# Sixteen product steps ahead of the gate matrices, their low halves by TensorE and ScalarE, and four of eight scaled one-hots on VectorE

## The chip, the cores and the metric

One of the eight cores of a Trainium2 chip runs the whole program. The metric is the device time of one execution in microseconds. The kernel before takes 2879.54 us (median of three runs, 2871.32 to 2884.39). The profiled execution, from which all rows are taken, took 2871.9 us.

## The reference, cut to what matters

A decoder block: two convolutional token mixers and a projection, then a layer of 16,384 single-neuron experts (PEER) for 1024 tokens of width 1024. Each token picks 16 experts for each of 8 heads, from the sums of two scores over 128 keys each.

```python
idx = e1 * PEER_N_KEYS + e2
gates = jax.nn.softmax(vals.astype(jnp.float32), axis=-1).astype(q.dtype)
u_sel = jnp.take(u, idx, axis=0)
act = jax.nn.gelu(jnp.einsum("chkd,cd->chk", u_sel, xc))
v_sel = jnp.take(v, idx, axis=0)
return jnp.einsum("chk,chkd->cd", act * gates, v_sel)
```

## The kernel before, in words

The front part makes the mixers, the normed tokens and, in `front`, the routing: VectorE picks the best 16 of 128 scores for every token and head. The tokens stand in eight tiles of 128. Three tiles are done by gathering: their experts' rows of u and v are fetched one by one. Five tiles (`ND`, 640 tokens) are done densely: all 128 chunks of 128 experts are multiplied with all 640 tokens, and a gate matrix, 0 where an expert was not picked, weighs the result.

`gate_matrix` makes these gates for a token as one product of two one-hot matrices: 128 picks by the 128 first keys, scaled with the gates (`o1`), and 128 picks by the 128 second keys (`o2`). It goes through each tile in 16 blocks of 8 tokens (`W`). For a block VectorE writes `o2` for all eight tokens (line 691, reading the transposed picks from PSUM). For the first `X` = 6 tokens VectorE writes unscaled bf16 one-hots `ob` (line 693), and ScalarE scales each token's by its gates (line 698). For the other two VectorE makes the scaled one-hot itself (line 700). TensorE multiplies (line 705; an fp32 product is two records in the trace), ScalarE copies the 128x512 result into `st` (line 708), and after 64 tokens SyncE stores `st` in DRAM, four transfers each. `o1`, `o2`, `ob`, `st`, `pa` have two buffers each, and so has the PSUM pool of the results (`pmm`). Ahead of a tile's blocks TensorE transposes its picks (lines 676, 678), and VectorE and ScalarE make the next tile's (`experts`, lines 498 to 535).

Beside the gates, TensorE makes the u products of 16 of the 128 chunks (`AHEAD`). `hidden_ahead` is a generator: a chunk is four steps (two halves of the width, two column ranges of 320 tokens), each of 12 products in three terms, high by high, low by high and high by low (`mm3`, lines 186 to 188). `prep_u` loads a chunk's u rows, transposes them on TensorE (line 733, PSUM pool `ptr`, two banks), ScalarE rounds them to the high half `uhi` (line 154), and VectorE subtracts that from the PSUM bank for the low half `ulo` (line 155). Behind a finished column range stands a Gelu on ScalarE (line 757) and a store (line 758). `gate_matrix` takes `LEAD` = 4 of the generator's steps before tile 0, 0.6 of a step (`RATE`) with each block of 8 tokens, and what is left after the last block:

```python
ahead, due = self.hidden_ahead(gm), 0.0
for _ in range(LEAD):
    next(ahead)
...
due += RATE
while due >= 1:
    next(ahead, None)
    due -= 1
...
for _ in ahead:
    pass
```

Then `token_experts` makes the picks of the three gathered tiles (line 545), and `dense` does the other 112 chunks with the gathered tiles' fetches between them. The gates are read back for two chunks at a time (line 801).

The program's order is not the order of the source: a scheduler puts each engine's instructions into one queue by priorities and expected readiness, and each queue is then taken strictly in that order. The products ahead use the four PSUM banks of pool `pms`, two for a chunk; the routing's scores and each tile's transposed picks use the same four.

Of the kernel before, what the change touches and what calls it, by code (L numbers as in the profile page):

```python
# [10 lines left out]
F32 = mybir.dt.float32  # L11
F32R = mybir.dt.float32r
# [9 lines left out]
P = 128  # L22
# [20 lines left out]
GB_T = 64  # L43
GB, LAG = 8, 6
AHEAD = list(range(5, NK, 8))
# [2 lines left out]
STEP = 4  # L48
AHD = 1
PACE = (2, 2, 2, 2, 1, 1, 1, 1, 1, 1)  # L50
LEAD = 4
HEAD = 4


def segments(n):
    m = -(-n // 512)
    step = -(-n // m)
    step += step % 2
    return [slice(i, min(i + step, n)) for i in range(0, n, step)]


class Block:
# [28 lines left out]
    def constants(self):  # L91
        nc, t, const = self.nc, self.t, self.const
        self.ident = self.tile(const, [P, P], F32, "ident")
        make_identity(nc, self.ident)
        self.identb = self.tile(const, [P, P], BF16, "identb")
        nc.scalar.copy(self.identb, self.ident)
        self.ones = self.tile(const, [P, P], F32, "ones")
        nc.vector.memset(self.ones, 1.0 / C)
        nrow = SCW + CFW + 5
        with self.pool("vec", 1) as vec:  # L100
            rows = self.tile(vec, [P, C], F32, "rows")
            nc.scalar.dma_start(rows[0:SCW], t["sc_conv_w"][0])
            nc.scalar.dma_start(rows[SCW:SCW + CFW], t["cf_conv_w"][0])
            for i, k in enumerate(("cf_conv_b", "cf_ln_g", "cf_ln_b", "out_norm_g_sc", "out_norm_g_cf")):
                r = SCW + CFW + i
                nc.scalar.dma_start(rows[r:r + 1], t[k][0:1])
            self.cols = self.tile(const, [P, 4, nrow], F32, "cols")
            ps = self.tile(self.ptr, [P, 4, P], F32, "tr")
            for c in range(4):
                nc.tensor.transpose(ps[:, c, :nrow], rows[:nrow, c * P:(c + 1) * P], self.ident[:nrow, :nrow])  # L110
            nc.vector.tensor_copy(self.cols, ps[:, :, :nrow])
        self.h_d = self.tile(self.dram, [SEQ, D], F32, "hd")
        self.x_d = self.tile(self.dram, [NG * P, D], F32, "xd")
        self.p_d = self.tile(self.dram, [len(AHEAD), P, ND * P], F32, "pd")
        self.g_d = self.tile(self.dram, [NK // 2, NK, ND * P // GB_T, 2, GB_T], F32, "gd")
# [538 lines left out]
    def gate_matrix(self, first, routes):  # L654

        nc, V = self.nc, self.nc.vector
        W, X, B = 8, 6, GB_T
        with self.pool("gm", 2, right=True) as gm:
            iota = self.tile(gm, [P, NK], F32, "iota", bufs=1)
            nc.gpsimd.iota(iota, pattern=[[1, NK]], base=0, channel_multiplier=0,  # L660
# [5 lines left out]
# [3 lines that stand above are left out]
            for n in range(ND):  # L669
# [4 lines left out]
                for l in range(2):  # L674
                    for m in range(TOPK):
                        nc.tensor.matmul(ps[:, l, :], oh[:, l * TOPK + m], self.identb,
                                         start=m == 0, stop=m == TOPK - 1)
# [7 lines left out]
                for q in range(P // W):  # L685
                    with self.tc.high_priority(offset=400 if n == 0 and q < HEAD else 0):
# [8 lines left out]
                        for m in range(W):  # L695
                            c = W * q + m
# [5 lines left out]
                        for z in range(W // 4):  # L702
                            pg = self.tile(self.pmm, [P, 512], F32, "mm").rearrange("p (e t) -> p e t", t=4)
                            for m in range(4):
                                nc.tensor.matmul(pg[:, :, m], o2[:, 4 * z + m, :], o1[:, 4 * z + m, :],  # L705
                                                 start=True, stop=True)
                            c = (W * q + 4 * z) % B
# [19 lines left out]
    def prep_u(self, c, q):  # L727
# [7 lines left out]
        self.split(*uT, ps)  # L735
        return uT

    def hidden(self, ps, uT, q, s):

        (hi, lo), (xh, xl) = uT, self.nT  # L740
        self.mm3(ps, (lambda a: hi[:, a, :], lambda a: lo[:, a, :]), (lambda b: xh[:, b, s], lambda b: xl[:, b, s]),
                 [(k, 4 * q + k) for k in range(4)], q == 0, q == 1)

    def hidden_ahead(self, pool):

        T = ND * P
        segs = segments(T)
        uT = self.prep_u(AHEAD[0], 0)
        for i, c in enumerate(AHEAD):
            pu = [self.tile(self.pms, [P, 512], F32, "ms")[:, :s.stop - s.start] for s in segs]  # L750
            for q in range(2):
                cur = uT
                for s, ps in zip(segs, pu):
                    self.hidden(ps, cur, q, s)
                    if q == 1:
                        p = self.tile(pool, [P, segs[0].stop], F32, "pa")[:, :s.stop - s.start]
                        self.nc.scalar.activation(p, ps, AF.Gelu_apprx_tanh)
                        self.nc.sync.dma_start(self.p_d[i, :, s], p)
                    if s is segs[0]:
                        if q == 0:  # L760
                            uT = self.prep_u(c, 1)
                        elif i + 1 < len(AHEAD):
                            uT = self.prep_u(AHEAD[i + 1], 0)
                    yield

    def dense(self, stream):
# [111 lines left out]
```

## Time and profile before

| | us |
|---|---|
| median of three runs | 2879.54 |
| profiled execution | 2871.9 |
| its span, first to last instruction | 2870.1 |
| TensorE busy (matmul records) | 2712.1 (94%) |
| TensorE weight loads | 2485.9 (87%) |
| VectorE busy | 2434.9 (85%) |
| ScalarE busy | 945.3 (33%) |
| GpSimd busy | 919.0 (32%) |

Busy shares are means over stages with different limits, so a stage is read in a view of windows. In the views PE is TensorE, PEld its weight loads, DVE VectorE, ACT ScalarE, POOL GpSimd and SP SyncE; PEclk is the clock that TensorE was granted as a share of full speed (2.4 GHz, or half of it, 1.2 GHz). A row of the timeline gives the start, the time taken by a run of equal instructions (xcount) and, in brackets, the idle time of the engine before it with what ended it. Matmul ends are modelled, so what a product costs in a burst is read from start to start.

### The profile page before, as it was taken

The numbers are of one execution on the slowest core, as the hardware profiler recorded it, in microseconds if no ns is written. First come the engines' busy times: TensorE is split into PE (matmuls) and PEld (weight loads), VectorE is DVE, ScalarE is ACT, GpSimd is POOL, SyncE is SP. The second block draws the span as 40 slices with busy tenths as digits, with TensorE's granted clock in tenths as the row PEclk, the third lists the DMA queues.
The fourth block names the chain that finished last, engine by engine and source line by source line (L and its number), as shares of the span: only waits on it lengthen the run. The fifth ranks groups of instructions, "written<-read, shape, count | busy, mean of one in ns | idle before, by whom it ended". The sixth has DMA issues, their size and how long they took to land.

```text
span 2870.1 us, 43789 instructions
## 1 busy us (share of the span) xinstructions
PE 2712.1 (94%) x16481; PEld 2485.9 (87%) x16481; DVE 2434.9 (85%) x5024; ACT 945.3 (33%) x1887; POOL 919.0 (32%) x793
## 2 busy tenths in 40 slices
PE   6999999986999989999999999999999999999998
PEld 6999989976888988898888889888888889888887
DVE  5998777998777569889889898889899988989986
ACT  4112431116999731222222212222222222222222
POOL 0000011110000025445544454445544544545440
PEclk9999999998999999999999999999999999999999
DMA  3112221101656789999989999999999999989992
GB/s 112 45 45 82 95 96 37 38 19 43 181 163 174 211 315 325 329 321 332 324 311 319 320 331 334 321 329 326 333 326 325 326 327 319 326 316 333 330 313 82
DMA packets 299540, 684.08 MB, mean 238 GB/s; under 512 B 20617, under 2 KB 153737, under 8 KB 299328
## 3 DMA queue, kind: packets, MB, share of 16 engines
q0 software_dynamic: 110592, 402.70, 39.4%
q1 hardware_dynamic: 188256, 276.92, 28.9%
q8 instruction: 130, 2.13, 0.3%
q10 hardware_dynamic: 480, 1.65, 0.1%
q14 instruction: 82, 0.67, 0.1%
HBM read 624.05 MB, written 57.15 MB: 237 GB/s over the span
## 4 chain that ended last, share of the span: by engine, by line
PE 64%; DVE 16%; ACT 9%; DMA 9%; issue 2%; SPq 0%; DVEq 0%; ACTq 0%
PE ms L188 12%; PE ms L187 12%; PE ms L186 12%; PE mm L188 7%; PE mm L186 7%; PE mm L187 7%; DMA raw<-in_peer_v_dram 7%; ACT o L698 4%; DVE row L637 3%; PE tr L733 2%; PE mm L705 2%; DVE vlo L155 2%; ACT st L708 2%; DVE g L611 1%; DVE s L467 1%
## 5 line engine op out<-in xcount | busy, mean ns | idle before, releaser
L588 POOL DMA_INDIRECT g<-in_peer_u_dram,ix x384 | 435.1, 1133 | 831.1 <-DVE ix L549 391.1
L186 PE MATMUL mm<-nhi,uhi 128*128 128x320 f32 x1792 | 573.1, 320 | 32.4 <-ACT p L824 32.0
L588 POOL DMA_INDIRECT g<-in_peer_v_dram,ix x384 | 440.6, 1147 | 455.1 <-DVE row L637 387.6
L188 PE MATMUL mm<-nhi,ulo 128*128 128x320 f32 x1792 | 557.7, 312 | 15.7 <-DVE ulo L155 15.1
L187 PE MATMUL mm<-nlo,uhi 128*128 128x320 f32 x1792 | 554.7, 310 | 0.0
L186 PE MATMUL ms<-vhi,phi 128*128 128x512 f32 x1280 | 501.4, 392 | 1.5 <-ACT phi L154 1.4
L188 PE MATMUL ms<-vhi,plo 128*128 128x512 f32 x1280 | 498.8, 390 | 0.0
L187 PE MATMUL ms<-vlo,phi 128*128 128x512 f32 x1280 | 498.7, 390 | 0.0
L637 DVE SCALAR_TENSOR_TENSOR row<-g,w,row 128x1024 f32<-128x1024 f32 x384 | 492.0, 1281 | 6.1 <-DMA row<-hd 4.7
L611 DVE SCALAR_TENSOR_TENSOR g<-g,row 128x1024 f32<-128x1024 f32 x384 | 464.5, 1222 | 0.0
L186 PEld LDWEIGHTS mm<-nhi,uhi 128*128 128x128 f32 x1792 | 338.4, 189 | 42.4 <-ACT p L824 40.3
L188 PEld LDWEIGHTS mm<-nhi,ulo 128*128 128x128 f32 x1792 | 337.5, 188 | 24.9 <-DVE ulo L155 23.9
L187 PEld LDWEIGHTS mm<-nlo,uhi 128*128 128x128 f32 x1792 | 338.7, 189 | 1.2
L154 ACT CAST phi<-p 128x320 fp32r<-128x320 f32 x256 | 116.4, 459 | 561.6 <-PE ms L187 340.8
L186 PEld LDWEIGHTS ms<-vhi,phi 128*128 128x128 f32 x1280 | 240.5, 188 | 51.0 <-ACT phi L154 2.4
L188 PEld LDWEIGHTS ms<-vhi,plo 128*128 128x128 f32 x1280 | 240.5, 188 | 50.6 <-DVE plo L155 0.5
L154 ACT CAST vhi<-raw 128x1024 fp32r<-128x1024 f32 x128 | 132.9, 1049 | 456.7 <-PE ms L188 316.5
L187 PEld LDWEIGHTS ms<-vlo,phi 128*128 128x128 f32 x1280 | 240.6, 188 | 49.0
L791 DVE TENSOR_TENSOR acc<-acc,ms 128x512 f32<-128x512 f32 x320 | 219.4, 685 | 34.7 <-PE ms L188 33.9
L155 DVE TENSOR_TENSOR ulo<-tr,uhi 128x512 fp32r<-128x512 f32 x256 | 175.4, 687 | 52.7 <-ACT uhi L154 51.8
L155 POOL TENSOR_TENSOR wlo<-wraw,whi 128x1024 fp32r<-128x1024 f32 x16 | 38.0, 2378 | 568.6 <-ACT whi L154 568.6
L154 ACT CAST uhi<-tr 128x512 fp32r<-128x512 f32 x256 | 149.4, 584 | 198.3 <-PE tr L733 195.9
(201 smaller groups left out, 4978.5 us busy)
## 6 DMA issues: line engine op xcount, KB each, us to landing
raw<-in_peer_u_dram SPq DMA_DIRECT2D x128, 512.0 KB
raw<-in_peer_v_dram SPq DMA_DIRECT2D x128, 512.0 KB
gd<-st SPq DMA_DIRECT2D x40, 1024.0 KB
g<-gd SPq DMA_DIRECT2D x64, 640.0 KB
wraw<-in_w_in_dram SPq DMA_DIRECT2D x20, 512.0 KB
wraw<-in_peer_w_q_dram SPq DMA_DIRECT2D x16, 512.0 KB
g<-in_peer_u_dram,ix POOLq DMA_INDIRECT x384
g<-in_peer_v_dram,ix POOLq DMA_INDIRECT x384
```

Source lines behind the costliest of these rows:

```text
L154: nc.scalar.copy(hi, src)
L155: self.mark(eng.tensor_tensor(lo, src, hi.bitcast(F32), op=OP.subtract))
L186: self.nc.tensor.matmul(ps, lh(a), rh(b), start=first and i == 0, stop=False)
L187: self.nc.tensor.matmul(ps, lh(a), rl(b), start=False, stop=False)
L188: last = self.nc.tensor.matmul(ps, ll(a), rh(b), start=False, stop=final and i == n - 1)
L588: self.nc.gpsimd.indirect_dma_start(out=g, out_offset=None, in_=self.t[table][0], in_offset=bass.IndirectOffsetOnAxis(ap=ix, axis=0))
L611: self.after(nc.vector.scalar_tensor_tensor(ut, ut, 1.0, b["x"], op0=OP.mult, op1=OP.mult, accum_out=b["act"][:, k:k + 1]))
L637: self.after(nc.vector.scalar_tensor_tensor(b["h"], b.pop(k), res[0][:, k:k + 1], b["h"], op0=OP.mult, op1=OP.add))
L698: nc.scalar.activation(o1[:, m, :], ob[:, :, m], AF.Copy, scale=eT[:, 2, c:c + 1])
L705: nc.tensor.matmul(pg[:, :, m], o2[:, 4 * z + m, :], o1[:, 4 * z + m, :], start=True, stop=True)
L708: nc.scalar.copy(st[:, :, c:c + 4], pg)
L791: self.mark(V.tensor_tensor(acc[:, i, dd], acc[:, i, dd], po, op=OP.add))
```

## The change

`LEAD` becomes 16, four whole chunks. The chunks ahead are prepared by a new function, `prep_ahead`: the same four transposes into a PSUM bank, ScalarE's rounded copy `uhi`, then a product of `uhi` with a negative identity that TensorE adds onto the same bank, so that the bank holds the low half, and a second ScalarE copy for `ulo`. VectorE has no part in it. `prep_u` stays as it is for the dense stage. And `X` becomes 4: of eight tokens ScalarE scales four, VectorE makes four, and `ob` has 512 columns where it had 768.

```diff
--- before.py
+++ after.py
@@ -48,7 +48,7 @@
 STEP = 4
 AHD = 1
 PACE = (2, 2, 2, 2, 1, 1, 1, 1, 1, 1)
-LEAD = 4
+LEAD = 16
 HEAD = 4
 
 
@@ -94,6 +94,8 @@
         make_identity(nc, self.ident)
         self.identb = self.tile(const, [P, P], BF16, "identb")
         nc.scalar.copy(self.identb, self.ident)
+        self.minus = self.tile(const, [P, P], F32R, "minus")
+        nc.scalar.mul(self.minus, self.ident, -1.0)
         self.ones = self.tile(const, [P, P], F32, "ones")
         nc.vector.memset(self.ones, 1.0 / C)
         nrow = SCW + CFW + 5
@@ -654,7 +656,7 @@
     def gate_matrix(self, first, routes):
 
         nc, V = self.nc, self.nc.vector
-        W, X, B = 8, 6, GB_T
+        W, X, B = 8, 4, GB_T
         with self.pool("gm", 2, right=True) as gm:
             iota = self.tile(gm, [P, NK], F32, "iota", bufs=1)
             nc.gpsimd.iota(iota, pattern=[[1, NK]], base=0, channel_multiplier=0,
@@ -735,6 +737,22 @@
         self.split(*uT, ps)
         return uT
 
+    def prep_ahead(self, c, q):
+
+        nc = self.nc
+        if q == 0:
+            self.raw = self.load("peer_u", c)
+        ps = self.tile(self.ptr, [P, 4, P], F32, "tr")
+        for k in range(4):
+            nc.tensor.matmul(ps[:, k, :], self.raw[:, (4 * q + k) * P:(4 * q + k + 1) * P], self.ident,
+                             is_transpose=True, start=k == 0, stop=k == 3)
+        hi, lo = (self.tile(self.de, [P, 4, P], F32R, "u" + s, bufs=3) for s in ("hi", "lo"))
+        flat = lambda x: x.rearrange("p a b -> p (a b)")
+        nc.scalar.copy(hi, ps)
+        nc.tensor.matmul(flat(ps), self.minus, flat(hi), start=False, stop=True, skip_group_check=True)
+        nc.scalar.copy(lo, ps)
+        return hi, lo
+
     def hidden(self, ps, uT, q, s):
 
         (hi, lo), (xh, xl) = uT, self.nT
@@ -745,7 +763,7 @@
 
         T = ND * P
         segs = segments(T)
-        uT = self.prep_u(AHEAD[0], 0)
+        uT = self.prep_ahead(AHEAD[0], 0)
         for i, c in enumerate(AHEAD):
             pu = [self.tile(self.pms, [P, 512], F32, "ms")[:, :s.stop - s.start] for s in segs]
             for q in range(2):
@@ -758,9 +776,9 @@
                         self.nc.sync.dma_start(self.p_d[i, :, s], p)
                     if s is segs[0]:
                         if q == 0:
-                            uT = self.prep_u(c, 1)
+                            uT = self.prep_ahead(c, 1)
                         elif i + 1 < len(AHEAD):
-                            uT = self.prep_u(AHEAD[i + 1], 0)
+                            uT = self.prep_ahead(AHEAD[i + 1], 0)
                     yield
 
     def dense(self, stream):
```

What the scheduler makes of it is shown at three places. Lines from 96 on are two to eighteen higher in the changed file: 676 became 678, 698 became 700, 705 became 707, 733 became 747 in `prep_ahead`, 757 became 775.

TensorE where tile 0's gates begin; `tr` are the transposed u, `ms` the banks of the products or of the transposed picks, `oh` the picks of tile 0. Before:

```order
L733 MATMUL tr_6635<-ident_75,raw_6633 128x128 x4
L733 MATMUL tr_6658<-ident_75,raw_6633 128x128 x4
L186 MATMUL ms_6644<-nhi_110,uhi_6640 128x320
L187 MATMUL ms_6644<-nlo_111,uhi_6640 128x320
L186 MATMUL ms_6645<-nhi_110,uhi_6640 128x320
L187 MATMUL ms_6645<-nlo_111,uhi_6640 128x320
L676 LDWEIGHTS oh_6426
L676 MATMUL ms_6348<-identb_80,oh_6426 128x128
```

and now, the end of the four chunks and the first transposes of the picks:

```order
L188 MATMUL ms_6882<-nhi_112,uhi_6900 128x320
L189 MATMUL ms_6882<-nlo_113,uhi_6900 128x320
L190 MATMUL ms_6882<-nhi_112,ulo_6901 128x320
L678 LDWEIGHTS oh_6428
L678 MATMUL ms_6350<-identb_80,oh_6428 128x128
```

Before, four of the first chunk's products stood ahead of the transposes of tile 0's picks, the other 44 behind. Now all 192 products of four chunks stand ahead, between the same score products of the routing and the same transposes.

ScalarE at the same place; `lst` and `pos` are what the picks of a tile are made from, `pi` and `pj` come from VectorE, `eT` are tile 0's transposed picks. Before:

```order
L518 CAST pos_6423<-pj_6405 128x8x16
L515 CAST lst_6772<-ind_439_3679 128x2x8x16
L682 COPY eT_6789<-ms_6348 128x384
L684 CAST e1b_6791<-ms_6348 128x128
L530 ACTIVATE gate_6781<-gate_6781 128x128
L517 CAST pos_6774<-pi_6755 128x8x16
L698 ACTIVATE o_926_6795<-ob_6797,eT_6789 128x128 x2
```

and now:

```order
L517 CAST lst_7011<-ind_440_3681 128x2x8x16
L751 CAST uhi_6822<-tr_6817 128x512
L519 CAST pos_7013<-pi_6994 128x8x16
L775 ACT_TABLE_LOAD
L775 ACTIVATE pa_6695<-ms_6647 128x320
L775 ACTIVATE pa_6722<-ms_6648 128x320
L753 CAST ulo_6823<-tr_6817 128x512
L751 CAST uhi_6861<-tr_6856 128x512
L520 CAST pos_7013<-pj_6995 128x8x16
L532 ACT_TABLE_LOAD
L532 ACTIVATE gate_7020<-gate_7020 128x128
L775 ACT_TABLE_LOAD
```

The cast from `pi_6994` (tile 1's positions, VectorE's) stands ahead of the first chunk's two Gelus, of a low half for the third chunk and of a high half for the fourth; between here and `eT` the order switches the table seven times. Outside this place the numbers of ScalarE's scaled one-hots fall from 480 to 320 and VectorE's rise from 160 to 320.

TensorE at the end of the gate stage; `mm` with `o` are gate matrices, `mm` with `identb` the picks of the first gathered tile. Before:

```order
L705 MATMUL mm_9984<-o_1509_9972,o_1508_9971 128x128
L705 MATMUL mm_9990<-o_1509_9972,o_1508_9971 128x128 x4
L187 MATMUL ms_10015<-nlo_111,uhi_9967 128x320
L188 MATMUL ms_10015<-nhi_110,ulo_9968 128x320
L186 MATMUL ms_10015<-nhi_110,uhi_9967 128x320
```

and now:

```order
L707 MATMUL mm_10235<-o_1539_10223,o_1538_10222 128x128
L189 MATMUL ms_10097<-nlo_113,uhi_10115 128x320
L707 MATMUL mm_10241<-o_1539_10223,o_1538_10222 128x128
L190 MATMUL ms_10097<-nhi_112,ulo_10116 128x320
L707 MATMUL mm_10241<-o_1539_10223,o_1538_10222 128x128 x3
L547 LDWEIGHTS identb_80
L547 MATMUL mm_10303<-oh_10291,identb_80 128x128
```

Before, 140 products and their transposes of u follow the last gate matrix, ahead of line 545. Now the last products of the sixteenth chunk alternate with the last gate matrices, and line 547 (545 before) follows at once. From there on the queues are the same in both programs but for single places.

## Rows read from the trace of the kernel before

**Rows 1.** Windows of the four stretches around the change: length, busy time of each engine

```profile
core 0: us, PE busy (x) PEld busy (x) DVE busy (x) ACT busy (x) POOL busy (x), PEclk, DMA share, GB/s
646.00:675.00 29.00, 9.34 (x54) 8.61 (x55) 27.33 (x181) 7.58 (x11) 0.00 (x0) 0.62 0.13 43
...
675.00:985.00 310.00, 289.64 (x2134) 263.50 (x2133) 235.47 (x472) 302.30 (x734) 0.00 (x0) 0.99 0.55 156
985.00:1008.00 23.00, 22.52 (x157) 21.97 (x155) 3.46 (x5) 5.23 (x11) 0.00 (x0) 1.00 1.00 295
1008.00:1033.00 25.00, 16.99 (x152) 16.24 (x152) 15.98 (x16) 9.19 (x14) 3.84 (x3) 0.80 0.82 305
```

**Rows 2.** ACT groups from 676 to 1010 us: xcount, busy us, mean ns, idle before

```profile
L698 ACT ACTIVATE o<-ob,eT 128x128 f32<-128x128 bf16 x480 | 186.2, 470 | 2.4 <-DVE ob L693 2.2
...
L154 ACT CAST uhi<-tr 128x512 fp32r<-128x512 f32 x30 | 17.6, 591 | 6.0 <-PE tr L733 6.0
...
L757 ACT ACT_TABLE_LOAD x6 | 7.7, 1283 | 0.1
```

**Rows 3.** Waits in the gate stage: who waited for whom, us, times, longest

```profile
DVE ob L693 <- ACT o L698: 41.4, 38, 2.5
PEld mm L705 <- ACT o L698: 23.3, 53, 1.9
```

**Rows 4.** Timeline of PE at the routing's end: start, us, what, idle before

```profile
646.21 1.94 PE L733 MATMUL tr<-ident,raw 128*128 128x128 f32 x8 [3.79 <-DMA raw<-in_peer_u_dram]
...
663.70 3.50 PE L676 MATMUL ms<-identb,oh 128*128 128x128 bf16 x32 [14.24 <-DVE s L467]
...
672.53 0.64 PE L188 MATMUL ms<-nhi,ulo 128*128 128x320 f32 x1 [5.21 <-DVE ulo L155]
```

**Rows 5.** Timeline of DVE at the same place and in the stage

```profile
671.79 0.69 DVE L155 TENSOR_TENSOR ulo<-tr,uhi 128x512 fp32r<-128x512 f32 x1
...
672.52 0.68 DVE L155 TENSOR_TENSOR ulo<-tr,uhi 128x512 fp32r<-128x512 f32 x1
...
674.67 0.29 DVE L502 SCALAR_TENSOR_TENSOR pi<-slot,pi 128x128 f32<-128x128 uint16 x1
...
675.12 2.35 DVE L691 TENSOR_TENSOR o<-iota,ms 128x1024 f32<-128x1024 f32 x2
...
698.50 1.11 DVE L700 TENSOR_SCALAR o<-iota,eT 128x128 f32<-128x128 f32 x4
699.52 1.02 DVE L693 TENSOR_TENSOR ob<-iob,e1b 128x768 bf16<-128x768 bf16 x2
```

**Rows 6.** Timeline of ACT at the start of the gate stage

```profile
675.04 0.76 ACT L517 CAST pos<-pi 128x128 bf16<-128x128 f32 x1
678.04 4.42 ACT L698 ACTIVATE o<-ob,eT 128x128 f32<-128x128 bf16 x12 [2.23 <-DVE ob L693]
682.34 0.58 ACT L708 COPY st<-mm 128x512 f32<-128x512 f32 x1
682.94 1.28 ACT L757 ACT_TABLE_LOAD   x1
684.23 0.44 ACT L757 ACTIVATE pa<-ms 128x320 f32<-128x320 f32 x1
```

**Rows 7.** Timeline of PE, last gate matrices and half a chunk of the tail

```profile
978.76 2.99 PE L705 MATMUL mm<-o,o 128*128 128x128 f32 x24
981.50 0.39 PE L186 MATMUL ms<-nhi,uhi 128*128 128x320 f32 x1
...
989.52 0.60 PE L733 MATMUL tr<-ident,raw 128*128 128x128 f32 x4
...
993.48 0.60 PE L733 MATMUL tr<-ident,raw 128*128 128x128 f32 x4
```

**Rows 8.** Timeline of SP's queue: the last gates' store and first read

```profile
985.29 10.58 SPq L716 DMA_DIRECT2D gd<-st  x4
...
1001.25 0.41 SPq L801 DMA_DIRECT2D g<-gd  x1
```

## The prediction

> **What bounds the kernel now.** I read the trace by stages first. The program has four stretches around the change [rows 1]: the end of the routing, 646 to 675 us, in which VectorE is busy (27.3 of 29.0 us), TensorE nearly idle (9.3 us) and its granted clock 0.62 of full speed; the gate stage, 675 to 985 us; a tail, 985 to 1008 us, in which TensorE alone works (22.5 of 23.0 us, VectorE 3.5, ScalarE 5.2); and from 1008 to 1033 us the experts of the last three tiles, before the dense stage. What follows, to 2870 us, has the same instructions before and after, so what the four stretches give is what the kernel gives.
>
> In the gate stage ScalarE is busy for 302.3 of 310 us [rows 1], 97.5%. TensorE shows 289.6 us, but its ends are modelled; VectorE shows 235.5 us. The costliest ScalarE group says with what: 480 scaled one-hots (line 698) [rows 2]. The waits agree: VectorE stands 41.4 us because ScalarE has not yet read a one-hot buffer, TensorE's weight loads stand 23.3 us for a scaled one-hot [rows 3]. ScalarE bounds this stage, TensorE bounds the tail, VectorE bounds the routing's end.
>
> **The routing's end.** TensorE has the first u chunk at 646.21, then stands 14.24 us until VectorE frees a PSUM bank for the gates' transposes, and 5.21 us more for the low half of u, a VectorE subtraction queued behind the routing [rows 4]. VectorE reaches its two subtractions at 671.79 and 672.52 [rows 5]. The change gives the low halves to TensorE and ScalarE, and puts four chunks where one stood. So 3 more chunks fill an idle TensorE. But queues are in order: the gates of tile 0 now stand behind all four chunks on TensorE, and on ScalarE the Gelus of the chunks stand behind a cast that waits for VectorE (second piece of order in the change's section).
>
> When does the gate stage begin? The source of that cast is ready at 674.67 + 0.29 [rows 5], less the two subtractions that go (0.60 us each from start to start): 673.5. From there ScalarE has in its order 2 position casts of 0.76 us, 8 Gelus and, priced like them, 3 exponentials of 0.44 [rows 6], 7 table loads of 1.28 and 7 casts of 0.59 [rows 2]: 1.5 + 4.8 + 9.0 + 4.1 = 19.4 us, to 693. TensorE needs these results, so it ends its chunks there, transposes the gates (3.5 us for 32 before [rows 4], some of it beside), and the first comparison starts near 695, where it started at 675.12 [rows 5]. **Term 1: +20 us.** Bounds: half a chunk (24 products, 4 transposes) takes 3.96 us when nothing else runs [rows 7], so eight take 32 us at full clock, to 678, with the transposes 682, +7; at half clock throughout, 63 + 3.5 us from 646, to 713, +38. I take the ScalarE sum, since its rows are nearest, and it lies between.
>
> The price of a table load I take as the trace has it: the copy before it starts at 682.34 and takes 0.58, the load starts at 682.94, the Gelu follows at 684.23 [rows 6], nothing else between. The Trainium skill (ScalarE: Activation LUTs, What ACT_TABLE_LOAD costs) puts a switch at about 2.66 us, 1.28 for the load and 1.38 for a drain; the load agrees, the drain shows in no row here. By that price the start would come 7 x 1.38 = 9.7 us later still, and the sum below would be 20 us instead of 30.
>
> **The gate stage.** Per eight tokens, two scaled one-hots leave ScalarE, two come to VectorE.
> - ScalarE: 12 of them took 4.30 us from start to start [rows 6], 0.36 each; 160 go: -57. 24 low-half copies come in the stage (the other 8 lie before it), priced as the high-half casts, 0.59 [rows 2], less some overlap: +13. About 3 table loads and some casts move ahead: -8. 302 becomes 250 us.
> - VectorE: four scaled one-hots took 1.02 us from start to start [rows 5], 0.255 each; 160 come: +41. The subtractions go (24 x 0.6: -14), routing work pulled ahead -9, and the bf16 one-hot over 512 columns instead of 768 (0.51 us each [rows 5]) saves between nothing and a third, 0 to 13. 235 becomes 240 to 253 us.
> - TensorE: 24 records (12 matrices) started in 2.74 us [rows 7], 0.228 each: 640 take 146. Twelve chunks of 7.9 us: 95. Gate transposes 8. The 24 subtractions by a negative identity are not in the trace; bounded by a 128x320 product and two of them (half a chunk's 3.96 us over 28 gives 0.14, so 0.14 to 0.28), near the upper for their 512 columns: 6. Sum 255 us.
>
> So the three engines come out at 250, 245 and 255, and none carries the stage alone. Bounds of its length: 257, if ScalarE is filled as it is now (250 / 0.975); 310, if the lighter ScalarE turns into waits elsewhere. I take **283**, where the engines are filled to 88 to 90%: below today's 97.5%, which one engine reached while the other two had a fifth or more to spare. **Term 2: -27 us.**
>
> **The tail.** 16 chunks are 64 steps. The stage advances 0.6 step per eight tokens, 48 steps for 640 tokens; before, 4 + 48 leave 12 steps, three chunks, for the tail; now 16 + 48 leave none, and the first expert transposes stand right behind the last gate matrix (third piece of order). **Term 3: -23 us** [rows 1].
>
> What hid behind the tail: the store of the last gates (10.58 us of issue from 985.29) and the first read of them, issued at 1001.25, 16 us after [rows 8]. Now their cover is the 25 us in which the three tiles' experts are made [rows 1]. That is enough, so they cost nothing. Were it not there, 16 us would come back. The negative identity at the start is one ScalarE instruction beside loads.
>
> **Sum.** 20 - 27 - 23 = **-30 us**. Against the profiled execution's 2871.9 us that is 2842. That execution lies 7.6 us below the median of the runs, 2879.5; the same change from the median gives **2850 us**.
>
> **The rivals.**
> - *Interlock.* With one-hots, gate banks and transposed blocks in two buffers each, three equally loaded engines wait for each other in turn. For it: 41.4 us of VectorE's waits already come from one two-deep buffer [rows 3]. Against it: TensorE has hidden products to put between. The stage takes 300 us, the sum is 20 - 10 - 23 = -13: 2866.
> - *The lead blocks the gates* (slower). TensorE takes its queue in order, so the gates can't start until four chunks, each with two round trips through ScalarE for hi and lo, are done. With the clock at the 0.62 of that stretch or below, start +38, and if then the stage is no shorter, +38 - 23 = +15: 2894. It decides once start and stage together exceed today's 333 us (675 to 1008). Against it: it takes the worst of both bounds.
> - *Better than forecast.* The start comes at +10, the stage runs in 262: 10 - 48 - 23 = -61: 2818.
>
> **How the numbers follow.** My forecast (20 to 45 us gained) 0.62; interlock 0.22 (6 to 20 us gained); the blocked start 0.07; better 0.09. A measurement can tell about 0.5%, 14.4 us, from no change. All of the forecast, the better case, and a third of the interlock lie beyond it: faster 0.78. The rest of the interlock and the milder blocked starts: same 0.17. Slower 0.05. The range takes terms 1 and 2 about half-way to their bounds: 13 - 40 - 23 = -50, 2830; 28 - 8 - 23 = -3, 2876.
>
> **What would show it.** Right: first comparison near 695; ScalarE below 92% in the gate stage, VectorE at 85% or more; last gate copy near 978, the expert transposes directly behind it, and every later event some 30 us earlier. Wrong: a start beyond 705; a stage over 300 us with all three engines below 85%; a read of the gates that the dense stage waits for; or a dense stage that has itself become longer.

## The result, and the profile after

The changed kernel takes **2841.96 us** (median of 4 runs, 2834.92 to 2844.79), the kernel before 2877.38 us beside it (median of 4): ratio **0.9868, interval 0.9847 to 0.9890**. The forecast was 2850, range 2830 to 2876, faster by over 0.5%. The time is inside, but two terms of the sum are off by 9 to 13 us, with opposite signs. The profiled execution (span 2838.8 us, before 2870.1) shows it.

Windows of the changed kernel in the columns of [rows 1]: the end of the routing with the lead, the gate stage, the experts with the start of the dense stage.

```profile
core 0: us, PE busy (x) PEld busy (x) DVE busy (x) ACT busy (x) POOL busy (x), PEclk, DMA share, GB/s
648.00:698.00 50.00, 43.78 (x275) 40.01 (x276) 33.26 (x208) 29.93 (x46) 0.00 (x0) 0.89 0.25 83
698.00:968.00 270.00, 265.58 (x2101) 252.95 (x2100) 240.84 (x576) 237.63 (x585) 0.00 (x0) 1.00 0.63 178
968.00:1004.00 36.00, 21.45 (x186) 20.15 (x183) 15.50 (x18) 9.03 (x16) 8.28 (x8) 0.85 0.99 333
```

The gate stage is 270 us instead of 310. ScalarE fell from 302 to 238 us, VectorE shows 241, and TensorE is busy for 265.6 of 270: 98%. There is no tail. In the third row the transfers are busy all the time (0.99), and TensorE works for 21 of 36 us.

TensorE's timeline around the end of the gates (start, duration, what, idle time before it and its releaser):

```profile
967.31 0.83 PE L707 MATMUL mm<-o,o 128*128 128x128 f32 x6
967.98 1.95 PE L547 MATMUL mm<-oh,identb 128*128 128x128 bf16 x32
...
983.46 3.24 PE L547 MATMUL mm<-oh,identb 128*128 128x128 bf16 x32 [4.13 <-DVE oh L526]
...
1005.38 1.09 PE L735 MATMUL tr<-ident,raw 128*128 128x128 f32 x4 [7.89 <-DMA raw<-in_peer_u_dram]
```

The experts' transposes (line 547) stand directly behind the last gate matrix, at 967.98 where they stood at 1008.13, 40.2 us earlier; what lay between, half a chunk at a time, is in [rows 7]. The span is only 31.3 us shorter. The last row shows most of the difference: TensorE stands 7.89 us for a chunk of u that has not arrived, a wait that the kernel before does not have.

The first comparison of VectorE, and ScalarE's queue ahead of it:

```profile
698.56 2.35 DVE L693 TENSOR_TENSOR o<-iota,ms 128x1024 f32<-128x1024 f32 x2
```

```profile
675.75 0.59 ACT L751 CAST uhi<-tr 128x512 fp32r<-128x512 f32 x1 [11.32 <-PE ms L189]
676.26 0.77 ACT L519 CAST pos<-pi 128x128 bf16<-128x128 f32 x1
677.05 1.28 ACT L775 ACT_TABLE_LOAD   x1
678.34 0.77 ACT L775 ACTIVATE pa<-ms 128x320 f32<-128x320 f32 x2
...
680.75 1.28 ACT L532 ACT_TABLE_LOAD   x1
682.05 0.31 ACT L532 ACTIVATE gate<-gate 128x128 f32<-128x128 f32 x1
...
697.48 0.48 ACT L684 COPY eT<-ms 128x384 f32<-128x384 f32 x1 [1.18 <-PE ms L680]
```

The start is 23.4 us later than in [rows 5]. The lead's first transpose is itself 2.0 us later (648.23 against 646.21 [rows 4]), a difference that lies ahead of the change; so the change moved the start by 21.4.

The gate stage's groups of the changed kernel (count, busy us, mean ns, idle before), one engine after the other:

```profile
L707 PE MATMUL mm<-o,o 128*128 128x128 f32 x1280 | 180.1, 282 | 4.0 <-ACT st L710 2.2 <-ACT o L700 1.5 <-DVE o L702 0.2
...
L752 PE MATMUL tr<-uhi,minus 128*128 128x512 f32 x23 | 10.9, 475 | 0.2 <-ACT uhi L751 0.2
```

```profile
L700 ACT ACTIVATE o<-ob,eT 128x128 f32<-128x128 bf16 x320 | 108.2, 408 | 1.9 <-PE mm L707 1.7
L710 ACT COPY st<-mm 128x512 f32<-128x512 f32 x159 | 90.5, 588 | 17.3 <-PE mm L707 16.9
```

```profile
L693 DVE TENSOR_TENSOR o<-iota,ms 128x1024 f32<-128x1024 f32 x80 | 97.1, 1219 | 11.5 <-PE mm L707 10.1
L702 DVE TENSOR_SCALAR o<-iota,eT 128x128 f32<-128x128 f32 x320 | 87.6, 343 | 0.0
L695 DVE TENSOR_TENSOR ob<-iob,e1b 128x512 bf16<-128x512 bf16 x80 | 31.4, 421 | 0.7 <-ACT o L700 0.6
```

TensorE's gate matrices in the kernel before, for comparison:

```profile
L705 PE MATMUL mm<-o,o 128*128 128x128 f32 x1280 | 194.4, 292 | 20.3 <-ACT o L698 10.8 <-ACT st L708 8.2
```

VectorE's 41.4 us of waiting for ScalarE's one-hots [rows 3] are 0.6 (line 695). ScalarE and VectorE wait for TensorE (16.9 and 10.1 us), and TensorE's gate matrices wait for anybody only 4.0 us, where they waited 20.3.

The theory for the experiments is theory P: since the change TensorE is what everything from the lead to the dense stage waits for, and behind the gates it is the transfers. The rival is the forecast's own view: no engine carries the stage alone, and the transfers cost nothing.

### The profile page after: what moved, and what is told of

It is laid out like the page before. It is cut to its first block, busy times and chain, and to the rows that moved or that the text cites. A ratio compares the mean times of both kernels' runs of the same rounds, so it can differ in the third digit from the quotient of the medians.

```text
span 2838.8 us, 43868 instructions
## 1 busy us (share of the span) xinstructions
PE 2700.6 (95%) x16513; PEld 2483.4 (87%) x16513; DVE 2443.3 (86%) x5152; ACT 897.6 (32%) x1764; POOL 913.7 (32%) x793
## 4 chain that ended last, share of the span: by engine, by line
PE 67%; DVE 16%; DMA 10%; ACT 4%; issue 2%; SPq 0%; DVEq 0%; ACTq 0%
PE ms L190 12%; PE ms L189 12%; PE ms L188 12%; DMA raw<-in_peer_v_dram 8%; PE mm L190 7%; PE mm L188 7%; PE mm L189 7%; PE mm L707 4%; DVE row L639 3%; DVE vlo L157 2%; PE tr L735 2%; DVE g L613 1%; DMA raw<-in_peer_u_dram 1%; DVE s L469 1%; ACT vhi L156 1%
## 5 line engine op out<-in xcount | busy, mean ns | idle before, releaser
L188 PEld LDWEIGHTS mm<-nhi,uhi 128*128 128x128 f32 x1792 | 337.9, 189 | 40.1 <-ACT p L842 38.4
L157 DVE TENSOR_TENSOR vlo<-raw,vhi 128x1024 fp32r<-128x1024 f32 x128 | 156.3, 1221 | 64.9 <-ACT vhi L156 64.8
L157 DVE TENSOR_TENSOR ulo<-tr,uhi 128x512 fp32r<-128x512 f32 x224 | 153.5, 687 | 43.5 <-ACT uhi L156 42.9
```

The lines of the kernel that those rows point to most:

```text
L157: self.mark(eng.tensor_tensor(lo, src, hi.bitcast(F32), op=OP.subtract))
L188: self.nc.tensor.matmul(ps, lh(a), rh(b), start=first and i == 0, stop=False)
```

## The experiments

Times of the profiled executions, in us. "Start" is the first comparison and "experts" the first of the experts' transposes, both counted from the lead's first transpose, so that what differs ahead of the change drops out; "rest" runs from the experts' transposes to the span's end. "Idle" is TensorE's idle time in the first 100 us of the rest, read from a window. The ratio is to the kernel before.

| kernel | start | experts | rest | idle | median | ratio (interval) |
|---|---|---|---|---|---|---|
| before | 28.9 | 361.9 | 1862.0 | 10.1 | 2877.4 | 1 |
| the change | 50.3 | 319.8 | 1870.8 | 16.8 | 2842.0 | 0.9868 (0.9847 to 0.9890) |
| no_x4 | 50.3 | 360.1 | 1870.2 | 16.2 | 2881.8 | 1.0007 (0.9995 to 1.0019) |
| no_low | 62.2 | 333.8 | 1875.9 | 15.4 | 2859.2 | 0.9936 (0.9918 to 0.9953) |
| no_lead | 34.4 | 323.3 | 1863.4 | 8.9 | 2835.3 | 0.9848 (0.9827 to 0.9869) |
| x4_only | 28.9 | 327.8 | 1877.1 | 10.8 | 2847.6 | 0.9892 (0.9871 to 0.9912) |
| rate45 | 50.3 | 317.7 | 1865.9 | 12.6 | 2830.9 | 0.9840 (0.9819 to 0.9860) |
| lead8_rate70 | 38.0 | 316.4 | 1867.9 | 16.5 | 2835.3 | 0.9864 (0.9841 to 0.9888) |
| lead8_rate55 | 38.5 | 320.9 | 1861.6 | 9.3 | 2831.4 | 0.9851 (0.9828 to 0.9874) |
| acc_late | 50.3 | 319.8 | 1869.7 | 15.7 | 2838.1 | 0.9867 (0.9849 to 0.9886) |
| late_gather | 50.3 | 319.7 | 1863.0 | 12.2 | 2831.9 | 0.9849 (0.9834 to 0.9864) |
| late_both | 50.3 | 319.7 | 1869.4 | 14.8 | 2839.8 | 0.9872 (0.9854 to 0.9891) |
| best | 38.0 | 316.3 | 1870.3 | 13.0 | 2834.2 | 0.9847 (0.9826 to 0.9868) |
| before_late_gather | 28.9 | 361.8 | 1865.7 | 8.8 | 2873.2 | 0.9987 (0.9974 to 1.0000) |

### Which part of the change does it

**no_x4**: the change with six scaled one-hots on ScalarE.

```diff
-        W, X, B = 8, 4, GB_T
+        W, X, B = 8, 6, GB_T
```

> The change with six of eight scaled one-hots on ScalarE again. ScalarE then has 238 us of the changed stage plus 160 x (0.39 to 0.47 us) = 300 to 313 us, so it sets the stage's length again: 303 to 318 us instead of 270, and the time is 2842 + 33 to 48, less the up to 8 us of the transfers' wait that such a longer stage hides: 2867 to 2890, not faster than the kernel before. Rival: ScalarE gives the low halves up late only where TensorE waits for them, and the stage stays within 285 (2855).

2881.8 us, no faster than before. Its window of the gate stage and ScalarE's costliest group there:

```profile
699.00:1009.00 310.00, 289.19 (x2105) 258.67 (x2104) 215.52 (x416) 305.73 (x746) 0.00 (x0) 0.99 0.55 158
```

```profile
L700 ACT ACTIVATE o<-ob,eT 128x128 f32<-128x128 bf16 x480 | 185.7, 468 | 0.6 <-DVE ob L695 0.3 <-ACT pa L775 0.2
```

ScalarE is busy for 305.7 of 310 us again, and the stage has its old length. Without this part the other two are worth nothing: the tail that they remove (23 us) pays for the later start (21 us), and the rest is 8 us longer, as in the change.

**x4_only**: the kernel before, with nothing changed but that number (6 to 4).

> The kernel before with four instead of six of eight scaled one-hots on ScalarE, and nothing else: no further steps ahead of the gates, low halves of u on VectorE. Theory P (TensorE is what the gate stage and the tail wait for, once ScalarE is relieved): VectorE has 241 + 23 x 0.69 = 257 us of the stage, TensorE 266 - 11 = 255, ScalarE 223; the stage starts at 675 as before, lasts 260 to 270, the tail of 23 us follows: the experts' transposes come at 958 to 968 instead of 1008, and with the tail as cover for the transfers nothing is given back behind it: 2828 to 2840, as good as the whole change or better. Rival S: the subtractions wait in VectorE's order behind comparisons of 1.2 us and a new 343 ns scaled one-hot each, TensorE waits for low halves in the stage as it did ahead of the gates (23 us) where the subtractions were left on VectorE with the longer lead, and the stage is 280 or longer: 2850 or more.

2847.6 us, so this one number brings 30 of the change's 35 us. It lies between the two expectations. The stage took 275 us, not 260 to 270, with TensorE busy for 98% of it and VectorE for 95%:

```profile
675.00:949.00 274.00, 267.35 (x2121) 255.41 (x2121) 259.20 (x627) 231.09 (x569) 0.00 (x0) 1.00 0.63 178
```

The rest was 15 us longer than in the kernel before. The first 100 us of it don't explain that (TensorE is idle for 10.8 us there, 10.1 before). Over the whole rest TensorE is idle for 76.7 us, 68.9 before, and busy 7.3 us longer with the same 10210 records. The granted clock was lower: behind 1030 us the sum of (1 - granted clock) over whole stretches of 10 us is 14.9 us here and 7.5 in the kernel before. So the 15 us lie scattered over the dense stage, half of them waits and half longer work. What brings them stays open; the profiled execution is the slowest of four, of which one took 2839.9 us at a mean clock of 0.988 and three took 2847.2 to 2852.5 us at 0.985.

**no_low**: the change with u's low halves by VectorE's subtraction.

```diff
-        uT = self.prep_ahead(AHEAD[0], 0)
+        uT = self.prep_u(AHEAD[0], 0)
...
-                            uT = self.prep_ahead(c, 1)
+                            uT = self.prep_u(c, 1)
...
-                            uT = self.prep_ahead(AHEAD[i + 1], 0)
+                            uT = self.prep_u(AHEAD[i + 1], 0)
```

> The change with u's low halves subtracted on VectorE, as before, for the chunks ahead as well. Theory P: the stage loses 23 products with minus (10.9 us of TensorE) and VectorE gains some 24 x 0.69 = 16.5 us, which makes it 257 of a stage of 270; the limit goes from TensorE (255) to VectorE (257), so the stage is 262 to 272 long and the time is 2834 to 2848. Rival D: in the routing's end VectorE is the busy engine, the eight subtractions of the lead (8 x 0.69 = 5.5 us) wait there behind one-hots that take 1.2 to 2.3 us each, and the gates start later by 6 to 15 us: 2848 to 2857.

2859.2 us, 17 us slower than the change: rival D, and a little more than it. TensorE's and VectorE's timelines of this kernel show the place:

```profile
673.97 0.63 PE L190 MATMUL ms<-nhi,ulo 128*128 128x320 f32 x1 [23.05 <-DVE ulo L157]
```

```profile
673.24 0.68 DVE L157 TENSOR_TENSOR ulo<-tr,uhi 128x512 fp32r<-128x512 f32 x1
```

The subtraction itself takes 0.68 us. It stands in VectorE's order behind the routing until 673.24, and all of the lead stands 23.05 us behind it on TensorE; the gates start 12 us later (62.2 against 50.3). The stage itself, up to the experts' transposes, is nearly as long as in the change (271.6 against 269.4 us). So the products with the negative identity are not there for the stage's sum: with the longer lead they take VectorE's queue out of its path.

**no_lead**: the change with `LEAD = 4`.

> The change without the twelve extra steps ahead of the gates (LEAD 4 again), with the minus products and with four of eight scaled one-hots on each engine. Theory P: in the changed kernel TensorE is the limit from the start of the lead to the experts' transposes (265.6 of the gate stage's 270 us), so the twelve steps cost it the same 23 us wherever they stand: the gate stage starts 20 us earlier, lasts 270 again, and the tail of 23 us alone is back, so the experts' transposes come at 968 to 972, where they come now (968). The transfers ahead of the dense stage then have the tail's 23 us to land in, and TensorE's wait of 7.9 us for the first dense chunk of u goes: 2832 to 2838. Theory F (the forecast's sum): start and tail cancel to 3 us, and the transfers cost nothing either way: 2845, that is 3 us slower than the change.

2835.3 us: theory P's figure, 7 us below the change, though the two ratio intervals overlap. The gates start 16 us earlier, and the stage is 262 us with TensorE busy for 257.9 of them:

```profile
682.00:944.00 262.00, 257.88 (x2045) 245.34 (x2044) 242.19 (x594) 241.20 (x588) 0.00 (x0) 1.00 0.64 181
```

The tail is back, the experts come 3.6 us later than in the change, and the rest is 7.4 us shorter: behind the last of the experts' transposes no wait of TensorE up to 1065 us is over 0.9 us. The lead of sixteen steps, on which the forecast's first and third terms rest, is thus no gain that shows in this kernel.

### Which engine holds the gate stage

**rate45**: the change with 36 steps beside the gates and twelve behind them.

```diff
-RATE = 0.6
+RATE = 0.45
```

> The change with 0.45 steps beside each eight tokens instead of 0.6: 36 beside the gates, and twelve alone behind them. Theory P: TensorE's 266 us beside the gates fall by 12 x 1.9 to 243, the stage with them until VectorE and ScalarE (241 and 238 us, less their share of twelve steps, some 9 us of ScalarE) hold it: 248 to 256 us, then a tail of 23: the experts' transposes come at 969 to 977, 1 to 9 us later than in the change, but the tail covers the transfers and the wait of 7.9 us is gone: 2834 to 2843. Rival (the forecast's view, that ScalarE and VectorE and not TensorE hold the stage): it stays at 268 to 270 and the tail comes on top: 2855 to 2862.

2830.9 us, 3 us below theory P's range and far below the rival's. Windows of its gate stage and of its tail with the first experts:

```profile
698.00:949.00 251.00, 248.09 (x1989) 236.07 (x1988) 239.55 (x576) 230.84 (x574) 0.00 (x0) 1.00 0.66 185
950.00:975.00 25.00, 20.46 (x162) 19.32 (x161) 6.06 (x7) 9.18 (x18) 0.00 (x0) 0.95 0.99 300
```

With twelve steps fewer the gates end at 947 instead of 968, while VectorE's work stays what it was (239.6 against 240.8 us). Up to the end of the gates TensorE is busy 20.5 us less and ScalarE 9.7 us less; the stage is 21 us shorter. So TensorE held the stage. TensorE shows 99%, VectorE now 95%: little is left to take away. Behind the tail of 19 us the wait of 7.9 us is gone: TensorE stands 3.42 us for a chunk of u among the experts' transposes, and behind the last of them no wait up to 1065 us is over 1.7 us.

**lead8_rate70** (`LEAD = 8`, `RATE = 0.7`) and **lead8_rate55** (`LEAD = 8`, `RATE = 0.55`):

> The change with eight steps ahead of the gates instead of sixteen and 0.7 steps for each eight tokens instead of 0.6 (56 beside the gates, so no tail either). Theory P: TensorE has 266 + 8 x 1.9 = 281 us beside the gates, the gates start some 5 to 13 us earlier than in the change (690 of a clean 696) and TensorE stays full: the experts' transposes come at 966 to 975 and the transfers give back the same 8 us: 2838 to 2848, no difference from the change. Rival: the idle 6 us of TensorE between 648 and 698 are what the long lead costs, and a shorter one saves them: 2832 to 2836.

> The change with eight steps ahead of the gates, 0.55 beside each eight tokens (44) and twelve alone behind the gates. The gates start 10 us earlier than with sixteen steps (as with eight steps and 0.7), TensorE has 8 x 1.9 = 15 us more beside them than with 0.45, and the tail of some 20 us covers the transfers as there. If the 3 us that the shorter lead saved up to the experts' transposes and the cover add, the transposes come 315 to 318 us after the lead's first transpose (317.7 with sixteen and 0.45) and the time is 2826 to 2830. Rival: once TensorE is full from the lead to the dense stage, the places of the steps exchange one for one: 2830 to 2834, no difference from sixteen and 0.45.

Eight steps ahead and none behind: the experts come at 316.4 instead of 319.8, and the wait for u is there as in the change (7.7 us). 2835.3 us is the rival's figure, but its interval lies about the change's. The stage is 278 us long with TensorE busy for 274.3 and VectorE for 237.9: with 36, 48 and 56 steps beside the gates (rate45, the change, this kernel) the stage grows with TensorE's work, and VectorE's does not. Eight ahead and twelve behind: experts at 320.9, the shortest rest of all (1861.6), 2831.4. Against rate45 the second expectation's rival holds: the places exchange one for one.

### What the transfers cost behind the gates

SyncE's queue of the changed kernel from the last gates' store on (start and time of issue):

```profile
968.79 9.62 SPq L718 DMA_DIRECT2D gd<-st  x4
978.51 3.61 SPq L819 DMA_DIRECT2D g<-gd  x1
982.21 3.40 SPq L797 DMA_DIRECT2D acc<-hd  x5
985.75 0.35 SPq L602 DMA_DIRECT2D row<-xd  x1
987.71 0.33 SPq L726 DMA_DIRECT2D raw<-in_peer_u_dram  x1
990.36 0.33 SPq L726 DMA_DIRECT2D raw<-in_peer_v_dram  x1
```

The chunk of u, the third of the dense stage, is issued at 987.71 and TensorE has it at 1005.38: 17.7 us for 512 KB. Over the whole profile the median is 6.3 (the page's DMA issues: count, KB each, us to landing):

```profile
raw<-in_peer_u_dram SPq DMA_DIRECT2D x128, 512.0 KB, 6.3
```

It is also issued late, 19.7 us behind the experts' first transpose, since the gates' store, their first read and the accumulator stand ahead of it in the queue. Its issue itself waited 1.5 us, by the profile for that read of the gates. In the kernel before the store goes out in the tail [rows 8], and the same chunk is issued 2.9 us behind the experts' first transpose, ahead of the accumulator:

```profile
1008.19 0.42 SPq L801 DMA_DIRECT2D g<-gd  x1
...
1011.00 0.33 SPq L724 DMA_DIRECT2D raw<-in_peer_u_dram  x1
1011.43 2.47 SPq L779 DMA_DIRECT2D acc<-hd  x5
```

The five kernels with a tail and unmoved loads (before, no_lead, x4_only, rate45, lead8_rate55) issue it 2.9 to 4.0 us behind that transpose, and TensorE is idle for 8.9 to 12.6 us in the first 100 us; the four without a tail (the change, no_x4, no_low, lead8_rate70) are idle for 15.4 to 16.8 us. In no_x4 and no_low the chunk is issued ahead of the last store and TensorE does not wait for it, but it then waits elsewhere (4.04 us in no_x4 for a Gelu that stands behind a chunk of v on ScalarE). So the order of the queue decides which load comes late, and without the tail some load does.

The chain of waits of the changed kernel goes through the chunk of v behind it:

```profile
988.52 0.32 PE mm L188
990.36 17.41 DMA raw<-in_peer_v_dram
1007.79 1.05 ACT vhi L156
```

**acc_late**: the accumulator's loads moved.

```diff
-            for i in range(ND):
-                nc.sync.dma_start(acc[:, i, :], self.h_d[i * P:(i + 1) * P])
...
+                if c == GRP - 1:
+                    for i in range(ND):
+                        nc.sync.dma_start(acc[:, i, :], self.h_d[i * P:(i + 1) * P])
                 if len(pend) == GRP:
```

> The change with the five loads of the accumulator (2.5 MB) issued at the fourth chunk of the dense stage, where they are first needed, instead of ahead of it. Theory T: between the last gates (968) and 1004 the transfers take all of the queues' time (0.99), the first dense chunks of u are behind the accumulator's 2.5 MB there (some 8 us at the 333 GB/s of that stretch), and TensorE's wait of 7.9 us for one of them is theirs: the wait goes to under 2 us and the time is 6 to 8 us shorter, 2834 to 2836. Rival G: the wait is the price of the eight gathers that start in the same stretch (4 MB), or the accumulator's loads cost the same 8 us where they now stand (the dense stage's transfers are busy 0.91): 2840 to 2844.

2838.1 us, between the two expectations, its interval on the change's. The chunk of u is issued 5.5 us earlier, counted from the experts' transposes. The wait for u is gone, and another has come (ScalarE's and TensorE's timelines of this kernel):

```profile
1016.51 1.04 ACT L156 CAST vhi<-raw 128x1024 fp32r<-128x1024 f32 x1 [8.04 <-DMA raw<-in_peer_v_dram]
```

```profile
1017.95 0.64 PE L188 MATMUL mm<-nhi,uhi 128*128 128x320 f32 x1 [6.14 <-ACT p L840]
```

ScalarE stands 8.04 us for a chunk of v, behind it on the same queue the Gelu that TensorE needs. The 2.5 MB cost nearly the same where they now stand (idle 15.7 against 16.8 us): the rival's second half.

**late_gather**: the first nine gathers and uses left out of the first three chunks' order (the stream's steps come later).

```diff
-            for _ in range(n):
+            for _ in range(n if go else 0):
                 next(stream, None)
...
+        go = False
...
             for c in range(NK):
+                go = c >= 3
```

> The change without the first nine gathers and their uses beside the first three chunks of the dense stage; they come nine steps later, where the order has some 26 steps to spare. The first eight gathers bring 4 MB, 12 us of the transfers' time at 333 GB/s, in the stretch of 968 to 1016 in which every transfer queue is busy. Theory G: these 12 us are what TensorE waits for (7.9 us before a chunk of u at 1005): the wait goes, 2833 to 2836. Rival: the first chunks of u are behind the gates' store and the accumulator's loads on SyncE's queue, which gathers don't share; the wait stays above 5 us and the time is 2840 to 2844.

2831.9 us, a little below theory G's range. But the edit did not do what its text says. The first eight gathers start at 987.22, in the change at 987.62: GpSimd's queue holds nothing ahead of them in either order. What moved is the load of `row` that belongs to them, now behind two chunks of u and one of v on SyncE's queue, the ninth gather (1037.6 instead of 1020.6) and VectorE's uses. SyncE's queue and TensorE's wait in this kernel:

```profile
984.96 0.33 SPq L726 DMA_DIRECT2D raw<-in_peer_u_dram  x1
986.63 0.33 SPq L726 DMA_DIRECT2D raw<-in_peer_v_dram  x1
...
990.33 0.33 SPq L726 DMA_DIRECT2D raw<-in_peer_u_dram  x1
991.86 0.33 SPq L602 DMA_DIRECT2D row<-xd  x1
```

```profile
1001.17 0.63 PE L735 MATMUL tr<-ident,raw 128*128 128x128 f32 x4 [3.12 <-DMA raw<-in_peer_u_dram]
```

Counted from the experts' transposes the chunk is issued 1.9 us earlier, and the wait falls from 7.89 to 3.12; the rest of the program is 7.8 us shorter. TensorE's idle time falls by 4.6 us in the first 100 us of the rest and by 5.6 us behind them. Which of the three moves did what beyond the wait was not separated. Theory G, that the eight gathers' 4 MB are the price, was not tried.

**late_both** (both edits), **best** (late_gather with `LEAD = 8`, `RATE = 0.7`), **before_late_gather** (late_gather in the kernel before):

> The change with both edits: the accumulator's 2.5 MB at the fourth chunk, the first nine gathers after the third. Together 6.5 MB, 20 us of the transfers' time at 333 GB/s, leave the stretch of 968 to 1016. If the bytes of that stretch are what costs the 8 to 9 us between the experts' transposes and the dense stage, no wait of over 2 us for a chunk of u or v is left on TensorE's path, and the time is 2831 to 2835. If what is taken out comes back as a wait in the next 50 us (as with the accumulator alone, where a wait of 6.1 us at 1018 took the place of the 7.9), it is 2838 to 2842.

> The change with eight steps ahead, 0.7 beside each eight tokens, and the first nine gathers after the third chunk of the dense stage. If the two edits act in different places (the shorter lead saved 3.4 us up to the experts' transposes, the later gathers 8 us between them and the dense stage), they add: 2826 to 2832, the fastest kernel of the study. Rival: with the experts 3 us earlier the transfers have 3 us less to land in, so the wait for a chunk of u comes back by as much: 2831 to 2836.

> The kernel before with the same later gathers. If the gain of the later gathers belongs to the wait for u's chunks, which the kernel before doesn't have (its tail of 23 us covers the transfers), it is nothing here: 2873 to 2881. Rival: gathers that start later help the dense stage in any case (fewer transfers in its first chunks, another order later): 2868 to 2872.

late_both is as slow as the change (2839.8), the second expectation's figure: waits of 2.4 and 3.9 us stand at 1004 and 1018, where acc_late alone has one of 6.1. best misses the sum: the experts come at 316.3, a wait of 4.5 us for u stands where late_gather has 3.1, and 2834.2 is the rival's figure. But the wait is only 1.4 us longer for experts that come 3.4 us earlier. In both profiles much of the long rest is longer work and no wait: over the rest TensorE is idle for 68.7 us (late_both) and 69.1 (best) against 77.3 in the change, but busy for 1800.7 and 1801.2 us against 1793.5 with the same 10210 records. In the kernel before, late_gather changes at most 0.3% (2873.2): its gain belongs mainly to the kernel without a tail. A small gain in the dense stage itself is not excluded.

The medians of three kernels are about 10 us below the change: rate45, lead8_rate55 and late_gather, which these runs don't tell apart. Their ratio intervals overlap the change's, too, so the order of the kernels below 2845 us is only indicated. All three leave the transfers behind the gates more time or a better order. rate45 changes one number of the change.

## Why the prediction was right or wrong

- **What bounds the stages: right.** no_x4 shows it for ScalarE in the gate stage: with 480 scaled one-hots on it the stage stays 310 us long, though the lead, the low halves and the missing tail are those of the change.
- **Term 1, the later start: right.** +20 forecast, +21.4 measured. ScalarE's queue from the position cast to `eT` took 21.2 us, 3.0 of them in three short waits for TensorE, against a sum of 19.4. That ScalarE's queue alone sets the start is not shown: from 678.8 to 694.6 TensorE is busy for 15.64 of 15.80 us and ScalarE for 13.79, and the profile's chain of waits runs through ScalarE up to 690.76 and through TensorE from there.
- **The table load: right.** 1.28 us each, and the next instruction starts 0.01 to 0.02 us after its end. The 1.38 us of drain in the Trainium skill (ScalarE: Activation LUTs, What ACT_TABLE_LOAD costs) show in none of the rows above either.
- **Term 2, the stage: right that relieving ScalarE shortens it, the size and the filling wrong.** -27 forecast, -40 measured (309.5 to 269.4 us). The step that failed is "the engines are filled to 88 to 90%". TensorE was filled to 98%. The hidden products between the gate matrices in its queue, the forecast's argument against the interlock, may be why, but no run took them out. And "none carries the stage alone" was wrong: rate45 shows that TensorE does. TensorE's sum was low as well, 255 us forecast against 265.6 busy, so the share filled was further off than the length shows. A smaller miss is ScalarE's sum, 250 forecast against 238: its scaled one-hots also became shorter (below).
- **Term 3, the tail: right as a term** (-23 us, experts directly behind the gates), **no gain together with term 1**. Work of TensorE moved from the tail into the lead costs it nearly the same time in both, so the lead's +21 and the tail's -23 are one and the same work. The forecast's own sum left 3 us of the two; the runs show 1.8 us up to the experts' transposes where ScalarE holds the stage (no_x4 against before) and 3.6 us where TensorE does (the change against no_lead), and the rest takes more back, 8.2 and 7.4 us.
- **"So they cost nothing": wrong.** The step counted the gates' store and their first read, and gave both the experts' 25 us as cover. It left out that the cover has other users: the accumulator's 2.5 MB, a chunk of u and one of v, `row`, and the first gathers, which in the kernel before come behind the tail too (1011.00 to 1028.40), but with the store already issued. From 968 to 1004 the transfers are busy 0.99, and the rest of the program became 8.9 us longer, 8.4 of them idle time of TensorE. So the premise that what follows the four stretches gives nothing failed with it. TensorE did not wait for a read of the gates itself, as the prediction's last part had it, but for a chunk of u that stands behind the store and that read in SyncE's queue.
- **The sum**: +23.4 (2.0 of it ahead of the change) - 40.1 - 23.5 + 8.9 = -31.3 us in the profiled executions, against -30 forecast; the medians differ by 35. The agreement is luck: two misses, -13 and +9, that nearly cancel.
- **The rivals**: no interlock (VectorE's wait for one-hot buffers vanished), no blocked start. With VectorE's subtraction left in place a blocked start does come, by another way than the rival's: 12 us in no_low, behind VectorE's queue.

## What to carry to other kernels

When a change takes the load off the engine that bounds a stage, work out which engine is next, and then count that engine's work over all stretches: moving its work from a tail into a lead is no gain for it. A stretch in which one engine works alone may be what covers the transfers of the stretch behind it, so before removing it add up all the bytes that land in it and in the stretch behind, and look at what stands ahead of the first needed load on its queue. Where a small operation of a busy engine feeds an idle one, its place in the queue (23 us here) can cost more than its time (0.68 us).

## What the runs showed of the hardware

- ScalarE's scaled copies read one column of a bf16 block [128, 128, X]. With X = 6 they take 468 to 470 ns (before and no_x4), with X = 4, the same output and number of elements, 406 to 408 (x4_only, the change and rate45). From start to start it is 0.36 us [rows 6] against 0.30 (eight in 2.52 us, less the last one's 0.41, over seven steps). The distance between the elements read differs, and so does what the other engines do meanwhile; no run varied it by itself.
- A 128x512 product with the negative identity takes 475 ns in the record. To the next product's start it is 0.33 us at 700.32; of the 27 single ones in the change at full clock with no wait right behind, 22 take 0.31 to 0.34 us, above the forecast's bound of 0.28, and five 0.22 to 0.24.
- In the dense stage the granted clock falls for a moment now and then. In the change TensorE stands 1.88 us up to 1589.48, and from 1591 to 1593 its clock is 0.50 (the lower level, 1.2 GHz); in x4_only it stands 3.05 us up to 1534.11, and the clock is 0.50 from there to 1540. Summed as above behind 1030 us, this comes to 1.7 us in the change's profile, 7.5 in the kernel before's and 15.3 in best's, on almost equal code. Single profiles of these kernels therefore don't rank two that are 5 us apart.
